# Attention in a one-core block kernel: PE's transposes, value products and halves of scores in another order at three places, two casts and one row scaling moved

## The chip, the cores and the metric

The kernel runs on one core of a Trainium2 chip. The metric is the device time of one execution in microseconds (us); of several executions the median is given. PE is the matmul engine (PEld its weight loads), DVE the vector engine, ACT the scalar engine, POOL and SP the two others; SP, POOL and ACT issue transfers. Each engine works through its own instructions in the order in which they were written, and waits on semaphores for the others.

## The reference

One layer of a block with two branches, for 1024 tokens of width 1024, in float32. What the change touches is the attention of branch A and the last product:

```python
h = rmsnorm(x, norm_g)
q, k, v, za, u, vs, zs, gm = split(h @ w_in)
q, k = partial_rope(q), partial_rope(k)            # 16 query heads, 2 key/value heads, 64 wide
s = einsum('bnqhgd,bnkhd->bhgnqk', qc, kb) / 8     # each chunk of 64 queries sees 192 keys
m = max(max(s), sink)
p = exp(s - m)
a = (p / (sum(p) + exp(sink - m))) @ vb            # 'bhgnqk,bnkhd->bnqhgd'
a = (a * silu(za)) @ w_att_out
sgo = (spatial_gating(gelu(u), gelu(vs)) * silu(zs)) @ w_sg_out
y = sigmoid(gm_a) * a + sigmoid(gm_s) * sgo
out = rmsnorm(x + y @ w_o, final_g)
```

## The kernel before

**The large products.** Every 1024-wide product is split two by two in Strassen's manner with seven partial products (weights' parts 0 to 6 against forms of the input called b11, t1, t2, b21, t3, b22, t4). Each float32 operand is held as a rounded high part and a rest (wh and wl for the weights; T_b11h, T_b11l and so on for the forms): ACT casts the high part (L174), DVE subtracts to get the rest (L175). One partial product (`product`, its matmuls at L388) is 12 matmuls of 128x512, three for each of four k. It takes a function `middle` that writes other work between k = 1 and k = 2. Accumulators lie in PSUM banks under four tags of two banks each: ps_mm, ps_o, ps_sc, ps_tp.

**Attention.** It has 32 steps (two key/value heads, eight blocks of 128 tokens, two parities). Eight locked pairs (`locked_pair`, p = 0 to 7) weave four steps each into the seven partial products of one pair of gate projections; the order of PE, ACT and DVE is there written out by hand and kept by the scheduler. In pair p the steps are called y and z (c and d of the pair before), then a, b, c, d. A step goes through these stages:

- `scores` (PE, L1196): two chunks of queries, each four matmuls of 128x192 into a ps_sc bank;
- `maxima` (DVE, L1221 to L1224), `exponentials` (ACT, L1231, L1240), `weigh` (DVE L1245 to L1252, ACT L1254): the normalised weights, tile pr;
- `turn` (PE): four transposes of the inner 128 keys (L1267) into one ps_tp bank, two of the outer 64-key ends (L1272) into another;
- `casts` (ACT, L1283, L1289), `inner_rest` (DVE, L1295), `ends_rest` (DVE, L1303): high parts and rests of the turned weights, tiles pT and pTb;
- `values` (PE, L1320): two matmuls of 128x512 with pT and two of 128x256 with pTb into a ps_o bank;
- `outputs` (ACT L1333, then DVE L1334): the result to tile aT, and from there to memory.

The pair begins with scores of a, turn of z, values of y on PE; then comes the b11 product, whose middle writes outputs of y, casts and rests of z, maxima and exponentials of a. Middle of t1: weigh a, values and outputs of z, the copy of the b11 accumulator to x11 (ACT, L1392), scores of b. The t2 product adds into that same accumulator, so it waits for the copy. Between t3 and b22: values of b, and then scores of d. At the end of a pair DVE adds t5 to x12 (L1471) and takes the rest of the next weights (L175), ahead of the next pair's outputs of y (L1334). Because only two ps_tp banks exist, the ends of z go into the bank that held the ends of y, and wait until `ends_rest` of y has read it.

In pairs 0 and 4 the first two steps belong to the first block of tokens, which has no earlier keys; their chunks are narrower. In pair 0 the scores of b come after the t1 product and not in its middle.

**The last product.** y @ w_o is done for four pairs of token tiles. Its seven forms are made from loaded quarters (tile bq) by `fill_b`; the last of them, t4, by two ACT casts T_t4h<-bq and two DVE rests. Around the same time `split_next` makes the weights' parts of the first token pair from tiles s and wr. PE first does the four b11 products, then, token pair by token pair, the other six.

**The last rows.** In the last token pair `last_by_halves` does the t4 product in two halves of 256 columns: each is added (L1810), squared and summed (ACT, L1812); then come the root, four short DVE operations (L147 to L152), the scaling and the stores. `scale_and_store(0)` scales the row tile that was finished before it: on ACT one half (L1835), on DVE the other (L1838), each followed by a store from SP.

Of the kernel before, what the change touches and what calls it, by code (L numbers as in the profile page):

```python
# [32 lines left out]
P = 128  # L33
# [3 lines left out]
HALF = 512  # L37
NT = S // P
HD = 64
# [15 lines left out]
def hybrid_tile(  # L55
# [29 lines left out]
    def bank(tag, dt=F32):  # L85
        return psum.tile([P, 512], dt, name=nm("ps_" + tag), tag="ps_" + tag, bufs=2)
# [46 lines left out]
    a_dr = scratch("a_dr")  # L133
    y_dr = scratch("y_dr")

    roots = []

    def stat():
        return mtile([P, 1], F32, "st1", 16)
# [27 lines left out]
    def split(hi, lo, src, minus=False):  # L167
        if minus:
            nc.scalar.mul(hi, src, -1.0)
            return nc.vector.scalar_tensor_tensor(  # L170
                lo, src, -1.0, hi.bitcast(F32), op0=ALU.mult, op1=ALU.subtract
            )
        else:
            nc.scalar.copy(hi, src)  # L174
            return nc.vector.tensor_sub(lo, src, hi.bitcast(F32))  # L175
# [198 lines left out]
    term = [None]  # L374
    LAST_OF_Q = 8

    def product(acc, part, form, fresh, middle=lambda: None, cols=slice(0, HALF)):
        wh, wl = part
        bh, bl = (v[:, :, cols] for v in form)
        for k in range(4):  # L380
            if k == 2:
                middle()
                half_done = mm
            ks = slice(k * P, (k + 1) * P)
            for n, (lt, rt) in enumerate(
                ((wh[:, ks], bh[:, k, :]), (wh[:, ks], bl[:, k, :]), (wl[:, ks], bh[:, k, :]))
            ):
                mm = nc.tensor.matmul(  # L388
                    acc,
                    lt,  # L390
                    rt,
                    start=fresh and k == 0 and n == 0,
                    stop=k == 3 and n == 2,
                    skip_group_check=True,
                )
        return half_done
# [410 lines left out]
    late = []  # L807
# [363 lines left out]
    def atile(shape, dt, tag, bufs):  # L1171
        return mtile(shape, dt, tag, bufs, pool)

    def window_of(t, c):

        return (64 * c, 64 * c + 192) if t else (P, P + 64 * (c + 1))
# [3 lines left out]
        first = (192, -64)[c]  # L1180
        return slice(first + lo, first + hi)

    def scores(n):

        g, t, par = steps[n]
        st = held[n] = SimpleNamespace(g=g, t=t, par=par)
        qt, kt = qT.pop(0), keys[g, t][0]
        q_of = qt[:].rearrange("p i (q c) -> p c (i q)", c=2)
        st.sc = []
        for c in range(2):  # L1190
            lo, hi = window_of(t, c)
            sc = bank("sc")[:].rearrange("p (i k) -> p i k", i=2)
            st.sc.append(sc)
            for i in range(2):
                for f in range(2):
                    nc.tensor.matmul(  # L1196
                        sc[:, i, lo:hi],
                        q_of[:, c, i * P : (i + 1) * P],
                        kt[:, f, lo:hi],
                        start=f == 0,  # L1200
                        stop=f == 1,
                    )
# [8 lines left out]
        st.pr = atile([P, 2, 384], F32, "pr", 2)  # L1211

    def sinks_of(st):
        return (v[:, 4 * st.g + st.par : 4 * st.g + st.par + 3 : 2] for v in (sink_sb, nsink_sb))
# [41 lines left out]
    def cols(c):  # L1256
        return slice(256 * c, 256 * c + 256)

    def turn(n):

        st = held[n]
        st.wide = wide = P if st.t else 64
        st.inner = bank("tp")
        for c in range(2):
            for i in range(2):
                at = (2 * c + i) * P
                nc.tensor.transpose(  # L1267
                    st.inner[0:wide, at : at + P], st.pr[:, i, place_of(c, 64 if st.t else P, 192)], ident[:]
                )
        st.ends = bank("tp")  # L1270
        for i in range(2):
            nc.tensor.transpose(st.ends[0:wide, i * P : (i + 1) * P], st.pr[:, i, P : P + wide], ident[:])  # L1272
# [30 lines left out]
            nc.vector.tensor_sub(st.b[lo, cols(c)], st.ends[hi, 0:256], st.b[hi, cols(c)].bitcast(F32))  # L1303

    def values(n):

        st = held[n]
        if st.par == 0:
            keys[st.g, st.t][3] = atile([P, 4, P], F32, "aT", 2)
        _, inner, ends, st.at = keys[st.g, st.t]  # L1310
        st.po = bank("o")
        vs = slice(st.par * HD, st.par * HD + P)
        if st.t:
            terms = [(inner[:, vs], st.a[:, i, :], slice(0, HALF)) for i in range(2)]
        else:
            terms = [(ends[:, 0, vs], st.a[:], slice(0, HALF))]
        for c in range(0 if st.t else 1, 2):
            terms.append((ends[:, c, vs], st.b[:, cols(c)], cols(c)))
        for i, (lt, rt, cs) in enumerate(terms):
            nc.tensor.matmul(  # L1320
                st.po[:, cs], lt, rt, start=i == 0, stop=i == len(terms) - 1, skip_group_check=True
            )

    def outputs(n):
# [22 lines left out]
    def locked_pair(p, finish):  # L1347
# [4 lines left out]
        def of(make, n, *rest):  # L1352
            if 0 <= n < len(steps):
                make(n, *rest)

        def multiply(acc, at, form, fresh, middle):
            pace[0] = product(acc, ready[n, at], hb[form], fresh, middle)
            part_of_early(1 if p < 5 else 2)

        n = done[0]  # L1360
# [26 lines left out]
        def h2():  # L1387
            of(weigh, a)
            of(values, z)
            of(outputs, z)  # L1390
            x11 = held["x11"] = xtile()
            nc.scalar.copy(x11[:], acc)  # L1392
# [378 lines left out]
    for p in range(4):  # L1771
# [30 lines left out]
        def last_by_halves():  # L1802

            nc.vector.tensor_add(xr[:, 2, :], xr[:, 2, :], acc)
            for c in range(2):
                cs = slice(c * 256, (c + 1) * 256)
                z = xr[:, 2, cs]
                half = bank("mm")[:, cs]
                product(half, ready[n, 6], ob["t4"], True, cols=cs)
                pace[0] = nc.vector.tensor_add(z, z, half)  # L1810
                ss = stat()
                nc.scalar.activation(bank("tp")[:, cs], z, AF.Square, accum_out=ss[:])  # L1812
                if c == 0:
                    sq[1] = based(ss, sq[1][0])
                else:
                    sq[1] = rstd_of(ss[:], 1.0 / D, sq[1])
            r = sq[1]
            row = slice((t + 1) * P, (t + 2) * P)
            v = scaled[1, 1][:]
            for c in range(2):  # L1820
                cs = slice(c * 256, (c + 1) * 256)
                z = xr[:, 2, cs]
                nc.vector.scalar_tensor_tensor(z, z, r[:], g_out[:, 0, cs], op0=ALU.mult, op1=ALU.mult)
                nc.scalar.mul(v[:, cs], v[:, cs], r[:])
                nc.sync.dma_start(out[row, cs], z)
                nc.scalar.dma_start(out[row, HALF + c * 256 : HALF + (c + 1) * 256], v[:, cs])

        def scale_and_store(i, p=p, t=t, xr=xr, sq=sq, scaled=scaled):
            r = sq[i]
            row = slice((t + i) * P, (t + i + 1) * P)  # L1830
            for e in range(2):
                z = xr[:, 2 * i + e, :]
                if (i, e) in scaled:
                    v = scaled[i, e][:]
                    nc.scalar.mul(v, v, r[:])  # L1835
                    nc.sync.dma_start(out[row, half_of(e)], v)
                    continue
                by_gain = nc.vector.scalar_tensor_tensor(z, z, r[:], g_out[:, e, :], op0=ALU.mult, op1=ALU.mult)  # L1838
# [137 lines left out]
```

## Time and profile before

| what | us |
|---|---|
| median of three runs | 921.0 (920.84 to 921.24) |
| the profiled execution | 921.45 |
| its span, first to last instruction | 919.7 |
| PE busy | 907.4 |
| DVE busy | 691.2 |
| ACT busy | 529.6 |
| the eight locked pairs, by PE's first scores of each | 332.6 to 562.7 |
| from one pair's scores to the next, pairs 2 and 3 | 29.5 |

The profile is one execution seen by the hardware. A row of its timeline has the start, the length, the engine, the source line, the operation, the tiles (out<-in), the shape and how many instructions were merged; in brackets stands idle time of the engine before it and what ended it. Matmuls overlap one another in these rows, since their ends are modelled: a 128x512 one is shown 0.39 long, but in an undisturbed run the next starts about 0.227 after it. So PE is read from start to start. The 1.7 us between the execution's time and its span lie before the first and after the last instruction.

### The profile page before, as it was taken

What the parts mean: (1) busy time and instruction counts of PE and PEld (TensorE: products, weight loads), DVE (VectorE), ACT (ScalarE), POOL (GpSimd) and SP (SyncE); (2) the same over time, 40 slices, a digit from 0 to 9 for tenths busy, and PEclk for the clock granted to TensorE, in tenths of its full rate; (3) what the DMA queues carried; (4) which work ended last, traced back from release to release, by engine and by line L of the source; (5) the groups of instructions that cost most, each with busy time, mean ns of one, the idle gap of its engine ahead of it and who ended that gap; (6) DMA issues with size and microseconds to landing.
All of it is one profiled execution on the core that took longest, in us unless ns stands there. A gap on an engine that the chain in (4) does not pass through costs nothing.

```text
span 919.7 us, 13199 instructions
## 1 busy us (share of the span) xinstructions
PE 907.4 (99%) x4296; PEld 749.4 (81%) x4296; DVE 691.2 (75%) x1233; ACT 529.6 (58%) x1058; POOL 141.9 (15%) x213
## 2 busy tenths in 40 slices
PE   8999999999999999999999999999999999999996
PEld 5888888888888888888888888888888888887885
DVE  6774776656678678777887788765599689579986
ACT  7942433334445456877778878444476475467443
POOL 1002222213011001222111110001110111210012
PEclk9999999999999999999999999999999999999999
DMA  7328788877788879999999994775568666998633
GB/s 241 122 97 217 172 150 185 177 186 212 242 270 260 270 249 328 266 241 260 255 344 246 266 246 144 284 252 179 173 204 304 226 206 179 282 322 271 206 115 114
DMA packets 129024, 206.10 MB, mean 224 GB/s; under 512 B 12634, under 2 KB 59738, under 8 KB 128956
## 3 DMA queue, kind: packets, MB, share of 16 engines
q1 hardware_dynamic: 107292, 146.27, 49.3%
q0 software_dynamic: 21376, 58.73, 27.2%
q8 instruction: 34, 0.56, 0.3%
q14 instruction: 34, 0.28, 0.1%
q10 hardware_dynamic: 288, 0.26, 0.1%
HBM read 148.46 MB, written 90.31 MB: 260 GB/s over the span
## 4 chain that ended last, share of the span: by engine, by line
PE 88%; DVE 4%; ACT 3%; DMA 3%; issue 1%; SPq 0%; ACTq 0%
PE ps_mm L388 40%; PE ps_o L388 24%; PE ps_mm L646 6%; PE ps_tp L388 4%; PE ps_sc L1196 2%; PE ps_o L1320 2%; PE ps_sc L388 2%; PE ps_tp L857 2%; PE ps_tp L646 1%; PE ps_sc L646 1%; PE ps_o L646 1%; PE ps_tp L1267 1%; ACT pr L1231 1%; PE ps_tp L1272 1%; ACT pr L1254 1%
## 5 line engine op out<-in xcount | busy, mean ns | idle before, releaser
L174 ACT CAST wh<-s 128x1024 fp32r<-128x1024 f32 (+1 forms) x78 | 77.9, 1002 | 78.9 <-PE ps_mm L388 25.4
L175 DVE TENSOR_TENSOR wl<-s,wh 128x1024 fp32r<-128x1024 f32 (+1 forms) x78 | 90.9, 1166 | 21.6 <-ACT wh L174 21.4
L175 DVE TENSOR_TENSOR wl<-wr,wh 128x1024 fp32r<-128x1024 f32 (+1 forms) x64 | 60.3, 944 | 53.0 <-ACT wh L174 53.0
L174 ACT CAST wh<-wr 128x1024 fp32r<-128x1024 f32 (+1 forms) x64 | 53.0, 829 | 77.2 <-PE ps_mm L388 33.7
L1231 ACT ACTIVATE pr<-ps_sc,sm 128x192 f32<-128x192 f32 (+2 forms) x128 | 51.2, 407 | 30.6 <-DVE sm L1222 22.0
L333 POOL DMA_DIRECT2D sums<-in_w_dram x48 | 36.6, 861 | 207.4 <-PE ps_mm L388 86.4
L388 PE MATMUL ps_o<-T_b22h,wh 128*128 128x512 f32 x148 | 59.3, 401 | 0.0
L388 PE MATMUL ps_o<-T_t1h,wl 128*128 128x512 f32 x148 | 58.0, 392 | 0.4 <-DVE wl L175 0.4
L388 PE MATMUL ps_o<-T_t1h,wh 128*128 128x512 f32 x148 | 58.3, 394 | 0.0
L388 PE MATMUL ps_o<-T_b22l,wh 128*128 128x512 f32 x148 | 57.8, 390 | 0.0
L388 PE MATMUL ps_o<-T_b22h,wl 128*128 128x512 f32 x148 | 57.7, 390 | 0.0
L388 PE MATMUL ps_o<-T_t1l,wh 128*128 128x512 f32 x148 | 57.7, 390 | 0.0
L388 PE MATMUL ps_mm<-T_t4h,wh 128*128 128x512 f32 (+1 forms) x144 | 55.8, 388 | 0.0
L388 PE MATMUL ps_mm<-T_t2h,wh 128*128 128x512 f32 x140 | 55.5, 396 | 0.0
L388 PE MATMUL ps_mm<-T_t4l,wh 128*128 128x512 f32 (+1 forms) x144 | 55.3, 384 | 0.0
L388 PE MATMUL ps_mm<-T_t4h,wl 128*128 128x512 f32 (+1 forms) x144 | 55.3, 384 | 0.0
L388 PE MATMUL ps_mm<-T_b11h,wh 128*128 128x512 f32 x140 | 55.2, 394 | 0.0
L388 PE MATMUL ps_mm<-T_t3h,wh 128*128 128x512 f32 x140 | 54.8, 391 | 0.0
L388 PE MATMUL ps_mm<-T_b11l,wh 128*128 128x512 f32 x140 | 54.7, 391 | 0.0
L388 PE MATMUL ps_mm<-T_b11h,wl 128*128 128x512 f32 x140 | 54.6, 390 | 0.0
L388 PE MATMUL ps_mm<-T_t3h,wl 128*128 128x512 f32 x140 | 54.6, 390 | 0.0
L388 PE MATMUL ps_mm<-T_t2h,wl 128*128 128x512 f32 x140 | 54.5, 390 | 0.0
(405 smaller groups left out, 2470.2 us busy)
## 6 DMA issues: line engine op xcount, KB each, us to landing
wr<-in_w_dram SPq DMA_DIRECT2D x80, 256.0 KB
sums<-in_w_dram POOLq DMA_DIRECT2D x24, 512.0 KB, 6.7
s<-sums SPq DMA_DIRECT2D x24, 512.0 KB
wr<-in_w_dram SPq DMA_DIRECT2D x16, 512.0 KB
q_hl<-qhl SPq DMA_DIRECT2D x16, 512.0 KB
q<-q_hl SPq DMA_DIRECT2D x64, 128.0 KB
y_dr<-x POOLq DMA_DIRECT2D x28, 256.0 KB, 6.5
sums<-in_w_dram POOLq DMA_DIRECT2D x24, 256.0 KB, 7.4
```

The source lines that it names most:

```text
L174: nc.scalar.copy(hi, src)
L175: return nc.vector.tensor_sub(lo, src, hi.bitcast(F32))
L333: return lambda: paced(nc.gpsimd.dma_start(dst, src, accum_op=op))
L388: mm = nc.tensor.matmul(acc, lt, rt, start=fresh and k == 0 and n == 0, stop=k == 3 and n == 2, skip_group_check=True,)
L646: mm = nc.tensor.matmul(acc, lt, rt, start=k == 0 and n == 0, stop=k == KC - 1 and n == 2)
L857: nc.tensor.matmul(pm[:, t * P : (t + 1) * P], xh[:, half * 4 + t, g * P : (g + 1) * P], bias[-1][1][:, g % 4, :], start=True, stop=True,)
L1196: nc.tensor.matmul(sc[:, i, lo:hi], q_of[:, c, i * P : (i + 1) * P], kt[:, f, lo:hi], start=f == 0, stop=f == 1,)
L1231: nc.scalar.activation(st.pr[:, i, place_of(c, lo, hi)], st.sc[c][:, i, lo:hi], AF.Exp, bias=st.nmax[:, c, i : i + 1], scale=-1.0, accum_o ...
L1254: nc.scalar.mul(v, v, st.inv[:, c, i : i + 1])
L1267: nc.tensor.transpose(st.inner[0:wide, at : at + P], st.pr[:, i, place_of(c, 64 if st.t else P, 192)], ident[:])
L1272: nc.tensor.transpose(st.ends[0:wide, i * P : (i + 1) * P], st.pr[:, i, P : P + wide], ident[:])
L1320: nc.tensor.matmul(st.po[:, cs], lt, rt, start=i == 0, stop=i == len(terms) - 1, skip_group_check=True)
```

## The change

At three places of a locked pair PE's instructions are put into another order; then two casts and one scaling are moved. No instruction is added or removed.

1. Start of a pair (pairs 1 to 7): turn of z and values of y are each cut in two, and the halves alternate: inner transposes of z, inner values of y, end transposes of z, end values of y.
2. Middle of t1 (pairs 1 to 7): the second chunk of scores of b moves from the middle to just before the last k, three matmuls later. The loads of queries that are issued with scores go with it.
3. After t3 (all pairs): the first chunk of scores of d moves between the inner and the end values of b. The second stays behind the end values.
4. The last product: the two casts T_t4h<-bq are ordered behind the cast of the weights that `split_next` made just before.
5. The last rows: `scale_and_store(0)` is called after the second half's sum instead of ahead of both halves.

The diff, with the cutting of `scores`, `turn` and `values` into two functions each left out where it only moves lines:

```diff
+            hi_casts.append(nc.scalar.copy(hi, src))
...
-    def product(acc, part, form, fresh, middle=lambda: None, cols=slice(0, HALF)):
+    def product(acc, part, form, fresh, middle=lambda: None, cols=slice(0, HALF), late=lambda: None):
...
+            if k == 3:
+                late()
...
+    def chunk_scores(n, c):
...
+        if c == 0:
+            held[n] = SimpleNamespace(g=g, t=t, par=par, q=qT.pop(0), sc=[])
...
+        if c == 0:
+            return
         if n + 3 < len(steps):
             qT.append(query_stage(*steps[n + 3]))
...
         of(scores, a)
-        of(turn, z)
-        of(values, y)
+        of(turn_inner, z)
+        of(inner_values, y)
+        of(turn_ends, z)
+        of(end_values, y)
...
             if p:
-                of(scores, b)
-
-        multiply(t5, 2, "t1", True, h2)
+                of(chunk_scores, b, 0)
+
+        def late2():
+            if p:
+                of(chunk_scores, b, 1)
+
+        multiply(t5, 2, "t1", True, h2, late2)
...
-        of(values, b)
+        of(inner_values, b)
+        of(chunk_scores, d, 0)
+        of(end_values, b)
         of(weigh, c)
...
-        of(scores, d)
+        of(chunk_scores, d, 1)
...
     split_next()
+    of_weights = hi_casts[-1]
     for _ in range(4):
         ob = next(fill)
+    for cast in hi_casts[-2:]:
+        after(cast, of_weights)
...
                 pace[0] = nc.vector.tensor_add(z, z, half)
+                if c:
+                    scale_and_store(0)
...
         by_b21()
-        scale_and_store(0)
         last_by_halves()
```

How PE's rows move at the start of pair 2 (place 1; ps_sc is scores of a, ps_tp the transposes of z, ps_o the values of y, ps_mm the b11 product). Before:

```order
L1196 MATMUL ps_sc_3651<-k_3373,q_3375 128x192 x4
L1267 MATMUL ps_tp_3664<-ident,pr_3575 128x128 x4
L1272 MATMUL ps_tp_3669<-ident,pr_3575 128x128 x2
L1320 MATMUL ps_o_3673<-pT_3608,vi_3359 128x512 x2
L1320 MATMUL ps_o_3673<-pTb_3610,v_3356 128x256 x2
L388 MATMUL ps_mm_3645<-T_b11h_143,wh_3553 128x512
```

Now:

```order
L1197 MATMUL ps_sc_3651<-k_3376,q_3378 128x192 x4
L1278 MATMUL ps_tp_3664<-ident,pr_3575 128x128 x4
L1338 MATMUL ps_o_3670<-pT_3608,vi_3359 128x512 x2
L1288 MATMUL ps_tp_3673<-ident,pr_3575 128x128 x2
L1346 MATMUL ps_o_3670<-pTb_3610,v_3356 128x256 x2
L390 MATMUL ps_mm_3645<-T_b11h_143,wh_3558 128x512
```

The two end transposes have moved behind the two inner value products. On DVE and ACT no instruction moves anywhere in the attention.

ACT's rows around the casts of form t4 in the last product (wh are weights' parts, g and x the copies out of PSUM). Before:

```order
L1758 COPY g_8159<-ps_sc_8158 128x512
L174 CAST T_t4h_8137<-bq_8134 128x1024
L174 CAST wh_8086<-s_8080 128x1024
L174 CAST wh_8090<-wr_8071 128x512
L174 CAST wh_8090<-s_8081 128x512
L174 CAST T_t4h_8137<-bq_8134 128x1024
L1758 COPY g_8174<-ps_mm_8173 128x512
L174 CAST wh_8119<-s_8081 128x512
L174 CAST wh_8119<-wr_8071 128x512
L1758 COPY g_8189<-ps_mm_8188 128x512
```

Now:

```order
L1795 COPY g_8159<-ps_sc_8158 128x512
L174 CAST wh_8086<-s_8080 128x1024
L174 CAST wh_8090<-wr_8071 128x512
L174 CAST wh_8090<-s_8081 128x512
L1795 COPY g_8174<-ps_mm_8173 128x512
L174 CAST wh_8119<-s_8081 128x512
L174 CAST wh_8119<-wr_8071 128x512
L174 CAST T_t4h_8137<-bq_8134 128x1024 x2
L1795 COPY g_8189<-ps_mm_8188 128x512
```

Both casts of t4 now stand behind all casts of the first token pair's weights, and still ahead of the fourth copy.

DVE's rows at the end (st are single columns for the root, bq the rows of the output). Before:

```order
L152 TENSOR_SCALAR st_1587_8782<-st_1586_8781,st_1585_8780 128x1
L1838 SCALAR_TENSOR_TENSOR bq_8675<-bq_8675,st_1587_8782,bq_8212 128x512
L1798 TENSOR_SCALAR st_1591_8810<-st_1589_8807,st_1578_8755 128x1
L1810 TENSOR_TENSOR bq_8675<-bq_8675,ps_mm_8814 128x256
L1799 TENSOR_SCALAR st_1592_8811<-st_1591_8810 128x1
L147 TENSOR_SCALAR st_1598_8833<-st_1594_8828,st_1592_8811 128x1
```

Now:

```order
L152 TENSOR_SCALAR st_1587_8782<-st_1586_8781,st_1585_8780 128x1
L1835 TENSOR_SCALAR st_1591_8806<-st_1589_8803,st_1578_8755 128x1
L1847 TENSOR_TENSOR bq_8675<-bq_8675,ps_mm_8810 128x256
L1836 TENSOR_SCALAR st_1592_8807<-st_1591_8806 128x1
L1877 SCALAR_TENSOR_TENSOR bq_8675<-bq_8675,st_1587_8782,bq_8212 128x512
L147 TENSOR_SCALAR st_1598_8833<-st_1594_8828,st_1592_8807 128x1
```

The scaling of the finished row (L1838, now L1877) stands behind the second half's sum (L1810, now L1847).

More of the change, by code (lines that the diff above doesn't have):

```diff
@@ L134, in hybrid_tile @@
     y_dr = scratch("y_dr")
-    roots = []
+    roots, hi_casts = [], []
     def stat():
@@ L173, in split @@
         else:
-            nc.scalar.copy(hi, src)
+            hi_casts.append(nc.scalar.copy(hi, src))
             return nc.vector.tensor_sub(lo, src, hi.bitcast(F32))
@@ L1181, in place_of @@
         return slice(first + lo, first + hi)
-    def scores(n):
+    def chunk_scores(n, c):
         g, t, par = steps[n]
[L1186 to L1202, printed above, removed]
+        if c == 0:
+            held[n] = SimpleNamespace(g=g, t=t, par=par, q=qT.pop(0), sc=[])
+        st, kt = held[n], keys[g, t][0]
+        q_of = st.q[:].rearrange("p i (q c) -> p c (i q)", c=2)
+        lo, hi = window_of(t, c)
+        sc = bank("sc")[:].rearrange("p (i k) -> p i k", i=2)
+        st.sc.append(sc)
+        for i in range(2):
+            for f in range(2):
+                nc.tensor.matmul(
+                    sc[:, i, lo:hi],
+                    q_of[:, c, i * P : (i + 1) * P],
+                    kt[:, f, lo:hi],
+                    start=f == 0,
+                    stop=f == 1,
+                )
+        if c == 0:
+            return
         if n + 3 < len(steps):
@@ L1211, in scores @@
         st.pr = atile([P, 2, 384], F32, "pr", 2)
+    def scores(n):
+        for c in range(2):
+            chunk_scores(n, c)
     def sinks_of(st):
@@ L1259, in turn, with turn_inner @@
     def turn(n):
+        turn_inner(n)
+        turn_ends(n)
+    def turn_inner(n):
         st = held[n]
@@ L1269, in turn, with turn_ends @@
                 )
+    def turn_ends(n):
+        st = held[n]
+        wide = st.wide
         st.ends = bank("tp")
@@ L1305, in values, with inner_values @@
     def values(n):
+        inner_values(n)
+        end_values(n)
+    def inner_values(n):
         st = held[n]
@@ L1313, in values, with end_values @@
         if st.t:
-            terms = [(inner[:, vs], st.a[:, i, :], slice(0, HALF)) for i in range(2)]
+            terms = [(inner[:, vs], st.a[:, i, :]) for i in range(2)]
         else:
-            terms = [(ends[:, 0, vs], st.a[:], slice(0, HALF))]
+            terms = [(ends[:, 0, vs], st.a[:])]
+        for i, (lt, rt) in enumerate(terms):
+            nc.tensor.matmul(st.po[:], lt, rt, start=i == 0, stop=False, skip_group_check=True)
+    def end_values(n):
+        st = held[n]
+        ends = keys[st.g, st.t][2]
+        vs = slice(st.par * HD, st.par * HD + P)
         for c in range(0 if st.t else 1, 2):
-            terms.append((ends[:, c, vs], st.b[:, cols(c)], cols(c)))
-        for i, (lt, rt, cs) in enumerate(terms):
             nc.tensor.matmul(
-                st.po[:, cs], lt, rt, start=i == 0, stop=i == len(terms) - 1, skip_group_check=True
+                st.po[:, cols(c)], ends[:, c, vs], st.b[:, cols(c)], start=False, stop=c == 1, skip_group_check=True
             )
@@ L1354, in of, with multiply @@
                 make(n, *rest)
-        def multiply(acc, at, form, fresh, middle):
-            pace[0] = product(acc, ready[n, at], hb[form], fresh, middle)
+        def multiply(acc, at, form, fresh, middle, late=lambda: None):
+            pace[0] = product(acc, ready[n, at], hb[form], fresh, middle, late=late)
             part_of_early(1 if p < 5 else 2)
```

## The prediction

> **What bounds the kernel now.** I read the page's fourth part, the chain that ended last, then the answer on waits for the locked pairs, then the chain of waits, then the timeline at each place of the change, and last the granted clock.
>
> ```profile
> PE 88%; DVE 4%; ACT 3%; DMA 3%; issue 1%; SPq 0%; ACTq 0%
> ```
>
> PE's own work sets the end nearly everywhere, and no matmul is removed. So the change can only take away gaps between PE's starts, and these are small. The waits of PE's weight loads between 330 and 575 us (columns: total us, times, longest) name three places, the three that the change reorders:
>
> ```profile
> PEld ps_tp L1272 <- issue: 2.0, 5, 0.4
> PEld ps_o L1320 <- ACT sm L1240: 2.0, 6, 0.3
> PEld ps_sc L1196 <- ACT pr L1231: 1.2, 6, 0.2
> ```
>
> These are waits of the loader, partly under a running matmul, so they are a bound and no sum. The chain of waits, asked for 355 to 450 us, says more. Between two of the five L1272 stops it runs through ACT and DVE alone:
>
> ```profile
> 363.60 0.59 ACT aT L1333
> ...
> 391.94 0.41 PE ps_tp L1272 x2
> ```
>
> From the outputs of y in pair 1 to the ends' rest of y that PE's end transposes await in pair 2 there are 28 us of ACT and DVE handing work to each other. So in this part PE is tied once per pair to a second clock, the loop of ACT and DVE. Whoever shortens only PE's side shortens nothing until the loop gets shorter too. This is the question for each edit.
>
> **Place 1, start of a pair.** Pair 2 in the timeline:
>
> ```profile
> 391.13 0.60 PE L1267 MATMUL ps_tp<-ident,pr 128*128 128x128 f32 x4
> 391.83 0.69 DVE L1471 TENSOR_TENSOR x<-x,ps_o 128x512 f32<-128x512 f32 x1
> 391.94 0.41 PE L1272 MATMUL ps_tp<-ident,pr 128*128 128x128 f32 x2 [0.22 <-DVE pTb L1303]
> 392.11 0.71 PE L1320 MATMUL ps_o<-pT,vi 128*128 128x512 f32 x2
> 392.43 1.22 DVE L175 TENSOR_TENSOR wl<-s,wh 128x1024 fp32r<-128x1024 f32 x1
> 393.09 0.58 ACT L1333 COPY aT<-ps_o 64x512 f32<-64x512 f32 x1 [0.91 <-PE ps_o L1320]
> 393.71 0.68 DVE L1334 TENSOR_TENSOR aT<-aT,ps_o 64x512 f32<-64x512 f32 x1
> ```
>
> The end transposes wait for DVE's ends' rest of y (L1303), which ends just before L1471 starts at 391.83. The four inner ones began at 391.13 and need 0.46 (as the scores of place 3 below, 0.93 / 8 = 0.116 each), so the others could have gone at 391.59: PE stands 0.35. In the new order the two inner value products, 2 x 0.23, fill that stop, and as they no longer come behind it, the values of y end about 0.45 sooner.
>
> What does that buy? The outputs (ACT L1333) start sooner, but the next link is DVE's L1334, and DVE is not free: behind the rest it has L1471 (391.83) and L175 (392.43). How soon L1334 can follow L175 is shown at the end of the section, where the same three DVE steps stand as at a pair's start and nothing else held it:
>
> ```profile
> 567.65 1.22 DVE L175 TENSOR_TENSOR wl<-s,wh 128x1024 fp32r<-128x1024 f32 x1
> 568.78 0.68 DVE L1334 TENSOR_TENSOR aT<-aT,ps_o 64x512 f32<-64x512 f32 x1
> ```
>
> That is 1.13 from start to start; in pair 2 it is 393.71 - 392.43 = 1.28. So the loop shortens by at most 0.15, not by 0.45, and by 0.03 if L1334 has to see the end of L175 (1.22) first. I take 0.13, nearer to the row that shows the pair of steps unheld. Five stops, 5 x 0.13 = **0.65**.
>
> One pair differs. Pair 4 has no earlier keys for two of its steps, and at the start of pair 5 DVE waits for PE's side:
>
> ```profile
> 480.44 0.68 DVE L1334 TENSOR_TENSOR aT<-aT,ps_o 64x512 f32<-64x512 f32 x1 [0.34 <-ACT aT L1333]
> ```
>
> There up to 0.34 of PE's gain from pair 4 comes through; less some 0.1 for switches that pair 4 now makes without a wait to hide them: **0.25**.
>
> **Place 2, scores of b.**
>
> ```profile
> 397.02 0.62 PE L1320 MATMUL ps_o<-pT,vi 128*128 128x512 f32 x2
> 397.72 1.35 PE L1196 MATMUL ps_sc<-k,q 128*128 128x192 f32 x8
> 398.91 0.42 PE L388 MATMUL ps_o<-T_t1h,wh 128*128 128x512 f32 x1
> 400.32 0.59 ACT L1392 COPY x<-ps_mm 128x512 f32<-128x512 f32 x1
> 400.96 0.50 PE L388 MATMUL ps_mm<-T_t2h,wh 128*128 128x512 f32 x1
> ```
>
> Eight scores take 1.19 here (397.72 to 398.91), against 0.93 in place 3 (412.63 to 413.56): 0.26 of waiting for the exponentials of a to free the bank. The three matmuls between fill it. But six matmuls and six transposes later the t2 product starts at 400.96, 0.05 after ACT's copy to x11 ends (400.91): PE is caught there, and the copy hangs on the loop. I cost place 2 at **0**; the cover is that copy, and if it came sooner the six waits would give at most 6 x 0.26 = 1.6. The second chunk, 0.6 later, is read by DVE's maxima only after L1334; query loads issued with it are for three steps on.
>
> **Place 3, values of b and scores of d.**
>
> ```profile
> 411.78 0.62 PE L1320 MATMUL ps_o<-pT,vi 128*128 128x512 f32 x2
> 412.63 1.09 PE L1196 MATMUL ps_sc<-k,q 128*128 128x192 f32 x8
> 413.56 0.41 PE L388 MATMUL ps_o<-T_b22h,wh 128*128 128x512 f32 x1
> ```
>
> From 411.78 to 412.63 values take 0.85, against 0.70 where nothing holds them (397.02 to 397.72). The 0.15 goes, but PE carries it only to the next pair's end transposes, where the rest of y decides. In the last pair nothing waits for it any more: **0.1**. The new switches in pair 1 and the last cost as much: **-0.1**. Together the attention gives 0.65 + 0.25 + 0.1 - 0.1 = **0.9**. Ends: a loss of 0.2 if DVE gains nothing and switches count; 2.6 if PE's 0.45 came through at all five stops.
>
> A rule speaks against this part. The Trainium skill, "TensorE: Matmul & The Clock Gate", section "A second HAM failure mode: psum-queue depth-cycling", says that cycling through PSUM banks makes PE pause between groups so often that its clock gate swings between half and full rate. The change adds bank changes; it is rival 3 below.
>
> **The casts.**
>
> ```profile
> 841.36 0.68 DVE L1691 SCALAR_TENSOR_TENSOR s<-s,wr 128x512 f32<-128x512 f32 x1
> 843.73 1.05 ACT L174 CAST T_t4h<-bq 128x1024 fp32r<-128x1024 f32 x1 [2.37 <-DMA bq<-g]
> 844.68 1.04 ACT L174 CAST wh<-s 128x1024 fp32r<-128x1024 f32 x1
> 845.76 1.22 DVE L175 TENSOR_TENSOR wl<-s,wh 128x1024 fp32r<-128x1024 f32 x1 [1.98 <-ACT wh L174]
> 846.20 0.40 PE L388 MATMUL ps_o<-T_t1l,wh 128*128 128x512 f32 x1
> 847.04 0.50 PE L388 MATMUL ps_o<-T_t1h,wl 128*128 128x512 f32 x1 [0.44 <-DVE wl L175]
> 847.38 0.39 PE L388 MATMUL ps_o<-T_t1h,wh 128*128 128x512 f32 x1
> ```
>
> ACT stands idle for a load of t4's source, with the weights' cast behind it, though s was done at 841.36 + 0.68 = 842.04. In the new order that cast runs 842.1 to 843.1, DVE, idle for 1.98 ahead of 845.76, takes the rest at about 843.8, and it ends by 845.1. PE wants it at 846.43 and finds it: 847.04 - 846.43 = 0.61, and the restart after the stop (847.38 - 847.04 = 0.34 for 0.23) gives 0.11: 0.72. DVE is then 1.5 or more ahead, which also removes the next such stop:
>
> ```profile
> 863.27 0.39 PE L388 MATMUL ps_o<-T_t1l,wh 128*128 128x512 f32 x1
> 863.53 0.50 PE L388 MATMUL ps_o<-T_t1h,wl 128*128 128x512 f32 x1
> ```
>
> 0.26 for a step of 0.23, and the same restart of 0.11: 0.14. Sum **0.86**. The price: t4's casts now come at about 847.3 to 849.3, behind the weights' casts, which wait for a buffer until the b11 products end near 846. Their reader, DVE's rest of t4, stands nine DVE steps behind the weights' first rest (845.76 before), each of some 0.6 to 1.2, so I expect room. Ends: 0 (if the buffer for the first cast is not free at 842) and 0.9.
>
> **The last rows.**
>
> ```profile
> 912.20 0.28 PE L388 MATMUL ps_mm<-T_t4h,wl 128*128 128x256 f32 x1
> 912.24 0.75 DVE L1838 SCALAR_TENSOR_TENSOR bq<-bq,st,bq 128x512 f32<-128x512 f32 x1
> 912.29 0.72 ACT L1835 ACTIVATE g<-g,st 128x512 f32<-128x512 f32 x1 [0.25 <-DVE st L152]
> 913.03 0.41 DVE L1810 TENSOR_TENSOR bq<-bq,ps_mm 128x256 f32<-128x256 f32 x1
> 913.47 0.39 ACT L1812 ACTIVATE ps_tp<-bq 128x256 f32<-128x256 f32 x1 [0.46 <-DVE bq L1810]
> 914.01 0.21 DVE L147 TENSOR_SCALAR st<-st,st 128x1 f32<-128x1 f32 x1 [0.51 <-ACT ps_tp L1812]
> ```
>
> PE's last matmul ends at 912.20 + 0.28 = 912.48, and its sum could start at about 912.52; it runs at 913.03, since L1838 stands before it. Moved behind, it lets the square start at about 912.98 (ACT's L1835 ends at 913.01) for 913.47. L1838 then runs 912.95 to 913.70, where DVE waits anyway (0.51 ahead of L147); it delays L147 by under 0.2, which ACT's root next to it covers. I take **0.45**; ends 0 and 0.5. Its store goes out 0.7 later, still over a microsecond ahead of the last ones.
>
> **Sum.** 0.9 + 0.86 + 0.45 = 2.2. The profiled execution took 921.45, so it becomes 919.25; it lies 0.45 above the median of 921.0, which becomes **918.8**.
>
> **Rivals.**
>
> 1. *PE's side comes through* (0.13): DVE's L1471 and L175 turn out not to hold L1334. For it: ACT stands 0.91 idle ahead of L1333 at 393.09. Against: DVE's start to start of 1.28 in pair 2 is full already. 5 x 0.45 + 0.25 + 1.31 = 3.8: 917.2.
> 2. *The attention's waits only move* (0.20): the ends' rest, the x11 copy and the loop take back all, and the edit there does nothing that it says. For it: PE's starts at 391.94 and 400.96 both follow the awaited step within 0.14. Only 0.86 + 0.45 = 1.3 remain: 919.7.
> 3. *Slower* (0.04): PE's granted clock falls in the attention, as its groups get shorter and change banks more often. The row of the 201.7 us from pair 1 on:
>
> ```profile
> 361.00:562.70 201.70, 200.56 (x1078) 169.13 (x1077) 163.39 (x402) 157.11 (x460) 39.35 (x51) 1.00 0.98 261
> ```
>
> The granted clock (third from the end) is 1.00 with ten bank changes a pair already, which speaks against it. It decides below 2.2 / 201.7, a mean of 0.989; at 0.97 it costs 6.2, so 921.0 + 6.2 - 2.2 = 925.0. This is what the skill's rule on cycling would make of it; the trace does not agree with the rule so far.
>
> 4. *The casts give nothing* (0.05): the buffer of the first weights' cast is not free at 842. 0.9 + 0.45: 919.65.
>
> **How the numbers follow.** My forecast has 0.58, with 0.5 either way. About 0.2% (1.8 us, so 919.2) is what a measurement of this kernel tells from no change. Of the forecast three quarters lie below 919.2, and all of rival 1: 0.57. Rivals 2 and 4 and the rest of the forecast lie within 0.2%: 0.38; slower 0.05. The range reaches to rival 1 and past rival 2: 917.0 to 920.1.
>
> **What would show it.** Right: no stop ahead of the end transposes, yet pairs 2 and 3 still about 29.35 apart, L1334 at 1.13 to 1.15 behind L175; t2 still 0.05 behind the x11 copy; no PE stops near 846 and 863; the last square about 0.5 nearer to PE's end. Wrong: pairs at 29.0 (rival 1) or 29.5 (rival 2), the rest still late at 846, or a granted clock under 1.00.

## The result and the profile after

| | median us | lowest to highest, runs |
|---|---|---|
| before | 921.02 | 920.62 to 921.96, 8 |
| changed | 918.99 | 916.94 to 920.57, 8 |

The ratio is 0.9979, with an interval of 0.997 to 0.9989: 1.0 to 2.8 us less, 2.0 by the medians. The forecast was 918.8.

The profiled execution of the changed kernel took 916.94, the lowest of its eight. So the two profiles lie 4.5 apart, and the stages have to be separated before anything is read from them. The marks are starts of PE's rows; pair 0 stands apart, since it took 25.6 to 26.4 in kernels that don't differ there. (PE's first scores of pair 0 start at 335.34 before; the 332.6 and 562.7 in the table further up are the starts of t4 products, so they are no marks of the pairs. The distances there are right.)

| stage, us | before | changed | less |
|---|---|---|---|
| up to PE's first scores of pair 0 | 335.34 | 333.39 | 1.95 |
| pair 0 | 25.77 | 25.59 | 0.18 |
| attention: first scores of pair 1 to the last end values | 210.23 | 209.28 | 0.95 |
| from there to PE's end (the casts lie here) | 341.14 | 340.21 | 0.93 |
| PE's end to the end of the span | 7.20 | 6.68 | 0.52 |

The first line is no part of the change: nothing before pair 0 was edited, and over all fourteen profiles of this study the first scores come between 333.39 and 337.16. What is left is 2.6 in this pair of profiles.

The chain that ended last, in the page of the changed kernel (share of the span by engine):

```profile
PE 84%; DVE 6%; ACT 5%; DMA 3%; issue 1%; SPq 0%; ACTq 0%
```

It was 88%, 4% and 3% before. PE was stopped less, yet a larger share of the chain runs through DVE and ACT. The waits of the locked pairs (330 to 575 us; total, times, longest) show where:

```profile
PEld ps_mm L390 <- ACT x L1420: 3.2, 6, 0.7
PE ps_mm L390 <- ACT x L1420: 1.6, 4, 0.4
PEld ps_tp L1288 <- issue: 1.3, 5, 0.3
```

The five waits of the end transposes on DVE (1.0 us of PE's own) and the six of the scores of b on ACT are gone from the list. In their place PE waits for ACT's copy of x11, which had been 0.2 us in one wait of the loader. Place 1 in pair 2, from the timeline:

```profile
388.89 0.60 PE L1278 MATMUL ps_tp<-ident,pr 128*128 128x128 f32 x4
389.25 0.71 PE L1338 MATMUL ps_o<-pT,vi 128*128 128x512 f32 x2
389.82 0.41 PE L1288 MATMUL ps_tp<-ident,pr 128*128 128x128 f32 x2
390.31 1.22 DVE L175 TENSOR_TENSOR wl<-s,wh 128x1024 fp32r<-128x1024 f32 x1
390.31 0.39 PE L390 MATMUL ps_mm<-T_b11h,wh 128*128 128x512 f32 x1
390.51 0.58 ACT L1359 COPY aT<-ps_o 64x512 f32<-64x512 f32 x1 [0.48 <-PE ps_o L1346]
391.44 0.67 DVE L1360 TENSOR_TENSOR aT<-aT,ps_o 64x512 f32<-64x512 f32 x1
```

In the kernel before, the first inner transpose of this pair starts at 391.13, and its b11 product here:

```profile
392.89 0.40 PE L388 MATMUL ps_mm<-T_b11h,wh 128*128 128x512 f32 x1
```

From the first inner transpose to the b11 product PE needs 1.42 (388.89 to 390.31), 1.76 before (391.13 to 392.89); in only_p1, further down, it is 1.36, so hardly a stop is left. ACT's output is done at 391.09, but DVE's part of it (L1360) starts at 391.44, which is 1.13 behind L175: DVE, busy with L175, is the one that holds it. And place 2, in the same pair:

```profile
396.32 0.60 PE L1197 MATMUL ps_sc<-k,q 128*128 128x192 f32 x4
397.91 0.38 PE L1288 MATMUL ps_tp<-ident,pr 128*128 128x128 f32 x2
398.02 0.59 ACT L1420 COPY x<-ps_mm 128x512 f32<-128x512 f32 x1
398.66 0.50 PE L390 MATMUL ps_mm<-T_t2h,wh 128*128 128x512 f32 x1 [0.37 <-ACT x L1420]
```

The scores of b no longer stop. PE comes to t2 sooner and stands there, until 0.05 after the copy ends (398.61), as before. The casts and the last row, from the timeline of ACT, DVE and PE:

```profile
839.00 1.05 ACT L174 CAST wh<-s 128x1024 fp32r<-128x1024 f32 x1 [0.72 <-DVE s L1725]
840.61 1.23 DVE L175 TENSOR_TENSOR wl<-s,wh 128x1024 fp32r<-128x1024 f32 x1
843.34 0.39 PE L390 MATMUL ps_o<-T_t1h,wl 128*128 128x512 f32 x1
843.56 0.39 PE L390 MATMUL ps_o<-T_t1h,wh 128*128 128x512 f32 x1
843.95 1.99 ACT L174 CAST T_t4h<-bq 128x1024 fp32r<-128x1024 f32 x2
848.69 1.24 DVE L175 TENSOR_TENSOR T_t4l<-bq,T_t4h 128x1024 fp32r<-128x1024 f32 x1
...
908.51 0.42 DVE L1847 TENSOR_TENSOR bq<-bq,ps_mm 128x256 f32<-128x256 f32 x1 [0.19 <-PE ps_mm L390]
908.92 0.74 DVE L1877 SCALAR_TENSOR_TENSOR bq<-bq,st,bq 128x512 f32<-128x512 f32 x1
908.97 0.39 ACT L1851 ACTIVATE ps_tp<-bq 128x256 f32<-128x256 f32 x1
909.57 0.21 DVE L147 TENSOR_SCALAR st<-st,st 128x1 f32<-128x1 f32 x1
```

The weights' rest ends at 841.84, 1.5 ahead of its reader at 843.34, and PE runs through in steps of 0.22 to 0.23. The casts of t4 end at 845.94; their reader on DVE starts at 848.69, so nobody waits. At the end the sum starts 0.03 after PE's last matmul ends (908.48), 0.55 before; the square and the scaling run beside one another.

### The profile page after: what moved, and what is told of

It is laid out like the page before. It is cut to its first block, busy times and chain, and to the rows that moved or that the text cites. A ratio compares the mean times of both kernels' runs of the same rounds, so it can differ in the third digit from the quotient of the medians.

```text
span 915.2 us, 13187 instructions
## 1 busy us (share of the span) xinstructions
PE 903.2 (99%) x4296; PEld 748.7 (82%) x4296; DVE 691.7 (76%) x1233; ACT 530.5 (58%) x1058; POOL 142.0 (16%) x213
## 4 chain that ended last, share of the span: by engine, by line
PE 84%; DVE 6%; ACT 5%; DMA 3%; issue 1%; SPq 0%; ACTq 0%
PE ps_mm L390 38%; PE ps_o L390 24%; PE ps_mm L648 6%; PE ps_tp L390 4%; PE ps_sc L390 2%; PE ps_tp L859 2%; PE ps_sc L1197 1%; ACT pr L1238 1%; DVE sm L1228 1%; PE ps_tp L648 1%; PE ps_sc L648 1%; PE ps_o L648 1%; ACT pr L1261 1%; DVE pTb L1319 1%; DMA q<-q_hl 1%
## 5 line engine op out<-in xcount | busy, mean ns | idle before, releaser
L175 DVE TENSOR_TENSOR wl<-s,wh 128x1024 fp32r<-128x1024 f32 (+1 forms) x78 | 91.1, 1168 | 20.3 <-ACT wh L174 20.0
L175 DVE TENSOR_TENSOR wl<-wr,wh 128x1024 fp32r<-128x1024 f32 (+1 forms) x64 | 60.6, 948 | 53.4 <-ACT wh L174 53.4
```

## The experiments

Twelve kernels, each timed in five to eleven executions beside the kernel before: only_... is the kernel before with that one part of the change, the others are the changed kernel with the edits shown below. "Pair 2" is the distance from PE's first scores of pair 2 to those of pair 3; the stages are those of the table above. A total carries the changing time up to pair 0, some 1 us either way for a median of five, so effects of less are read from the stages.

| kernel | median us | ratio to before, interval | pair 2 | attention | to PE's end | tail |
|---|---|---|---|---|---|---|
| before | 921.02 | | 29.50 | 210.23 | 341.14 | 7.20 |
| changed | 918.99 | 0.9979 (0.997 to 0.9989) | 29.32 | 209.28 | 340.21 | 6.68 |
| only_p1 | 920.4 | 0.9995 (0.9986 to 1.0004) | 29.37 | 209.25 | 340.93 | 7.19 |
| only_p2 | 920.98 | 1.0003 (0.9994 to 1.0012) | 29.52 | 210.39 | 340.71 | 7.20 |
| only_p3 | 920.81 | 0.9999 (0.9991 to 1.0008) | 29.51 | 210.48 | 340.20 | 7.19 |
| only_casts | 920.78 | 0.9997 (0.9988 to 1.0005) | 29.47 | 210.40 | 340.25 | 7.19 |
| only_tail | 920.6 | 0.9997 (0.9988 to 1.0006) | 29.55 | 210.33 | 340.91 | 6.69 |
| early | 918.73 | 0.9977 (0.9968 to 0.9986) | 29.33 | 209.00 | 340.21 | 6.68 |
| maxb | 915.63 | 0.9947 (0.9933 to 0.996) | 28.81 | 206.46 | 340.17 | 6.69 |
| maxb_early | 913.56 | 0.9925 (0.9913 to 0.9938) | 28.47 | 204.32 | 340.22 | 6.68 |
| me_none | 915.41 | 0.9939 (0.9927 to 0.9952) | 28.71 | 205.96 | 340.22 | 6.69 |
| me_no1 | 914.4 | 0.9931 (0.9918 to 0.9943) | 28.47 | 204.31 | 340.22 | 6.69 |
| me_no2 | 916.71 | 0.9945 (0.9931 to 0.9958) | 28.70 | 205.75 | 340.24 | 6.69 |
| me_no3 | 914.58 | 0.9929 (0.9917 to 0.9942) | 28.48 | 204.46 | 340.22 | 6.68 |

**One place at a time.** Place 1 alone, in the kernel before:

```diff
-        of(turn, z)
-        of(values, y)
+        of(turn_inner, z)
+        of(inner_values, y)
+        of(turn_ends, z)
+        of(end_values, y)
```

> The kernel before with place 1 alone (start of a pair: inner transposes of z, inner values of y, end transposes of z, end values of y). Theory (the loop of ACT and DVE limits the pair): the stop of 0.35 ahead of the end transposes is gone, but pairs 2 and 3 still take 29.36 (29.50 before) and pair 4 some 27.9 (28.15 before), in all 0.9 less: 920.1. Rival, PE's side comes through: pairs 2 and 3 take 29.05, in all 2.5 less: 918.5. Rival, the waits only move: 29.5, 921.0.

Pair 2 took 29.37, pair 3 29.34 and pair 4 27.73; attention 209.25, where the three kernels with an unchanged attention (before, only_casts, only_tail) have 210.23 to 210.40. That is 1.0 to 1.15 less, for 0.9 forecast; the total alone, with an interval that holds 1, would not have shown it. The timeline of pair 2 shows the second clock at work:

```profile
397.26 0.61 PE L1197 MATMUL ps_sc<-k,q 128*128 128x192 f32 x4
398.14 0.72 PE L1197 MATMUL ps_sc<-k,q 128*128 128x192 f32 x4 [0.27 <-ACT pr L1238]
398.69 0.41 PE L390 MATMUL ps_o<-T_t1h,wh 128*128 128x512 f32 x1
```

The scores of b take 1.43 (397.26 to 398.69) for 0.93 of work, a stop of 0.50, where it was 0.26. At the start of the pair PE saves 0.40 (1.36 from the first inner transpose, 391.07, to the b11 product, 392.43; 1.76 before). Of that it waits 0.24 more here; the rest, 0.16, is near the 0.13 by which the pair became shorter.

Place 2 alone:

```diff
-                of(scores, b)
-
-        multiply(t5, 2, "t1", True, h2)
+                of(chunk_scores, b, 0)
+
+        def late2():
+            if p:
+                of(chunk_scores, b, 1)
+
+        multiply(t5, 2, "t1", True, h2, late2)
```

> The kernel before with place 2 alone (second chunk of the scores of b three matmuls later). Theory: no gain, pairs 2 and 3 stay at 29.5, and the 0.26 saved stand as a stop of PE of 0.2 to 0.3 at the start of the t2 product, until ACT's copy of x11 ends: 921.0. Rival, the stop's time is gained: 6 x 0.26 = 1.6, pairs at 29.24, 919.4.

In the kernel before, the t2 product of pair 2 starts at 400.96, and the two end transposes ahead of it here:

```profile
400.76 0.38 PE L1272 MATMUL ps_tp<-ident,pr 128*128 128x128 f32 x2
```

With place 2:

```profile
401.42 0.59 ACT L1420 COPY x<-ps_mm 128x512 f32<-128x512 f32 x1
401.57 0.38 PE L1288 MATMUL ps_tp<-ident,pr 128*128 128x128 f32 x2
402.06 0.51 PE L390 MATMUL ps_mm<-T_t2h,wh 128*128 128x512 f32 x1
```

From the first of the two transposes to t2 it takes 0.49, where it was 0.20: a stop longer by 0.29, about the 0.26 that the scores no longer wait, and it ends 0.05 behind the end of the copy at 402.01. Pair 2 stays at 29.52. Place 3 alone:

```diff
-        of(values, b)
+        of(inner_values, b)
+        of(chunk_scores, d, 0)
+        of(end_values, b)
...
-        of(scores, d)
+        of(chunk_scores, d, 1)
```

> The kernel before with place 3 alone (first chunk of the scores of d between the inner and the end values of b). Theory: the 0.15 of PE's wait ahead of the end values goes, but the pairs with a stop at the next start (2, 3, 6) keep 29.5; only where no such stop follows (pairs 0, 1, 5 and 7) up to 0.15 each may show: 920.4 to 921.0. Rival, the time is gained in every pair: 29.35 in pairs 2 and 3 as well, 7 x 0.15 = 1.05, 919.9.

```profile
390.79 0.62 PE L1278 MATMUL ps_tp<-ident,pr 128*128 128x128 f32 x4
391.74 0.41 PE L1288 MATMUL ps_tp<-ident,pr 128*128 128x128 f32 x2 [0.33 <-DVE pTb L1319]
```

Pairs 1 and 5 became 0.14 and 0.15 shorter, as thought (the 0.18 of pair 0 shows nothing: it takes 25.61 in only_tail too, where it is unchanged). But in pair 2 PE then stands 0.14 longer at the next end transposes (0.95 from start to start here, 0.81 before), and pairs 3 and 4 took 0.27 and 0.14 more: over the attention nothing is left. In pair 3 of this kernel, and in the same pair of the changed one, PE also waits 0.22 at the inner transposes. In these two, and in maxb, ACT's scaling of the weights (L1261) waited once for DVE's L1259 instead of running beside it; why only there is open.

**The loop.** Two edits that leave PE's order alone. In the first ACT takes the copy of x11 where it was idle:

```diff
             of(exponentials, a, 0)
-            of(exponentials, a, 1)
 
         multiply(acc, 0, "b11", True, h0)
+        x11 = held["x11"] = xtile()
+        nc.scalar.copy(x11[:], acc)
+        of(exponentials, a, 1)
...
             of(outputs, z)
-            x11 = held["x11"] = xtile()
-            nc.scalar.copy(x11[:], acc)
```

> The changed kernel, and ACT's copy of x11 taken ahead of the second half of the exponentials of a, where ACT stood idle for 0.76; PE's order is untouched. Theory (the loop of ACT and DVE is the pair's second clock): PE's stop at the start of t2 (0.37 in pair 2) is gone, but it comes back as a stop later in the pair, at the transposes of b, and pairs 2 and 3 keep 29.2 to 29.3 (29.32 in the changed kernel): 918.5 to 919.0. Rival, this copy is what holds PE: six pairs gain 0.35 each, pairs 2 and 3 take 28.97, 2.1 less than the changed kernel: 916.9.

```profile
400.43 0.48 PE L390 MATMUL ps_mm<-T_t2h,wh 128*128 128x512 f32 x1
...
405.51 0.55 DVE L1259 TENSOR_SCALAR pr<-pr,sm 128x192 f32<-128x192 f32 x2
405.57 0.80 ACT L1261 ACTIVATE pr<-pr,sm 128x192 f32<-128x192 f32 x2 [0.50 <-DVE sm L1253]
405.97 0.78 PE L1278 MATMUL ps_tp<-ident,pr 128*128 128x128 f32 x4 [0.38 <-DVE pr L1259]
```

The stop at t2 is gone, and 5.5 us later PE stands 0.38 at the transposes of b, which wait for the weights (L1259, L1261). Pairs 2 and 3 take 29.33 and 29.31. A stop of 0.37 was taken away, and its whole length came back at the next meeting.

The second edit touches DVE's order alone (the small tiles of a step are also made with its first chunk instead of its second):

```diff
-            of(outputs, z)
-            x11 = held["x11"] = xtile()
-            nc.scalar.copy(x11[:], acc)
             if p:
                 of(chunk_scores, b, 0)
+                of(maxima, b, 0)
+            of(outputs, z)
+            x11 = held["x11"] = xtile()
+            nc.scalar.copy(x11[:], acc)
...
-        of(maxima, b, 0)
+        if p == 0:
+            of(maxima, b, 0)
         of(maxima, b, 1)
```

> The changed kernel, and on DVE alone the maxima of b's first chunk moved ahead of its part of the outputs of z, into 0.95 us in which DVE waits for ACT; PE's and ACT's orders are untouched. Theory (loop of ACT and DVE): ACT's exponentials of b come 0.6 to 1.0 sooner, the loop gets shorter, and PE gains though nothing of its own changed: pairs 2 and 3 take 29.0 to 29.1 (29.32 in the changed kernel), 0.8 to 1.2 less in all, 917.8 to 918.2. Rival, the loop is not what limits: pairs stay at 29.3, 919.0.

```profile
392.99 0.68 DVE L1360 TENSOR_TENSOR aT<-aT,ps_o 64x512 f32<-64x512 f32 x1 [0.46 <-ACT aT L1359]
...
398.58 0.55 DVE L1228 TENSOR_REDUCE sm<-ps_sc 128x2 f32<-128x384 f32 x1
399.60 0.59 ACT L1423 COPY x<-ps_mm 128x512 f32<-128x512 f32 x1
399.61 0.69 DVE L1360 TENSOR_TENSOR aT<-aT,ps_o 64x512 f32<-64x512 f32 x1 [0.29 <-ACT aT L1359]
400.08 0.43 ACT L1238 ACTIVATE pr<-ps_sc,sm 128x192 f32<-128x192 f32 x1
400.24 0.50 PE L390 MATMUL ps_mm<-T_t2h,wh 128*128 128x512 f32 x1
```

ACT's exponentials of b follow right behind the copy (399.60, then 400.08); in the changed kernel ACT stood idle for 0.99 between the copy, which ended at 398.61, and these:

```profile
399.60 0.42 ACT L1238 ACTIVATE pr<-ps_sc,sm 128x192 f32<-128x192 f32 x1 [0.99 <-DVE sm L1229]
```

And at the start of the pair (392.99) DVE's L1360 now waits 0.46 for ACT and PE, where it was late by itself: the loop is ahead of PE there. Pair 2 takes 28.81, 0.51 less, twice what was expected, and the total is 3.4 below the changed kernel, for 0.8 to 1.2 expected. The theory had the direction right, and its size was an estimate that was too small. Both edits together:

> The changed kernel with both: the maxima of b's first chunk ahead of the outputs of z on DVE, and the copy of x11 ahead of the second exponentials of a on ACT. Theory: with the loop shorter, the copy of x11 is what PE meets next, so the two together give more than the sum of each alone (at most 0.3 and some 1.0): pairs 2 and 3 at 28.8 to 28.9, 2.0 to 2.5 less than the changed kernel, 916.5 to 917.0. Rival, the two edits give what they give alone: 917.7.

Pair 2 at 28.47, 913.56: 0.9925 of before (0.9913 to 0.9938). That is again more than was expected (28.8 to 28.9, and 916.5 to 917.0). Early alone gave nothing on its own; behind maxb it gives 0.34 a pair, as the copy of x11 is then the last thing PE meets. The chain that ended last, in the page of this kernel:

```profile
PE 97%; DVE 1%; DMA 1%; ACT 0%; SPq 0%; issue 0%; ACTq 0%
```

and its windows row for the attention from pair 1 on, but for its last few us (the length of the window comes first, then PE's busy time; the granted clock is third from the end):

```profile
360.47:554.00 193.53, 193.53 (x1065) 166.77 (x1064) 162.06 (x400) 156.69 (x461) 38.58 (x50) 1.00 1.01 270
```

PE's rows leave no gap in all 193.53 us of it. This is the best version of the study.

**The three places again, with the loop out of the way.** In maxb_early each place was put back as it was before the change, and all three together (the same lines as in the diffs above, the other way round; casts and last row stay changed).

> The kernel with the maxima of b and the copy of x11 moved (maxb_early), and all three places of PE's order put back as they were before the change; casts and last row as in the changed kernel. Theory (the stops of before were made by the loop, which is shorter now): only the scores of b still wait for the exponentials of a, 0.1 to 0.2 a pair, and the switches of banks that the new orders add are saved; pairs 2 and 3 take 28.45 to 28.65 (28.47 with the new orders), 913.5 to 914.8. Rival, the stops are PE's own (0.35, 0.26 and 0.15 a pair as before): pairs take 29.2, 919.

> maxb_early with place 1 alone put back. Theory: the rest of y's ends ends at 389.70 there and PE's inner transposes end at 390.3, so the end transposes wait for nothing and pairs 2 and 3 stay at 28.4 to 28.5: 913.5. Rival: the stop of 0.35 comes back, pairs at 28.8, 915.5.

> maxb_early with place 2 alone put back. Theory: ACT's last exponential of a that frees the bank ends near 396.5, when PE would want it for the second chunk of the scores of b; a stop of 0.1 to 0.2 a pair, pairs 2 and 3 at 28.5 to 28.65, 913.9 to 914.8. Rival: 0.26 or more as before, pairs at 28.73 and 915.3; or none, 913.5.

> maxb_early with place 3 alone put back. Theory: the rest of b's ends ends at 409.04, PE wants it at 410.0, so nothing waits and pairs 2 and 3 stay at 28.4 to 28.5: 913.5. Rival: 0.15 a pair as before, pairs at 28.62, 914.6.

Pair 2 took 28.47 without place 1, 28.48 without place 3, 28.70 without place 2, and 28.71 without all three. So the worths are turned round: place 1, which alone paid in the change, is worth nothing here, and place 2, which was worth nothing there, is worth 0.23 a pair. In the waits of me_none (total, times, longest) there is one kind left of the three that stood in the profile before:

```profile
PEld ps_sc L1197 <- ACT pr L1238: 1.1, 6, 0.2
```

The scores of b wait for the bank that ACT's exponentials of a read, in all six pairs. That is a tie of its own between PE and ACT within a pair. The stops at the end transposes and at the values of b were only the loop being late. The expectation had 0.1 to 0.2 a pair for place 2, a little low, and the medians of all four lie above what was expected, by 0.6 to 1.9; part of that is the time up to pair 0 (337.16 in me_no2's profile, the latest of all).

**The casts and the last row alone.**

```diff
+    of_weights = hi_casts[-1]
     for _ in range(4):
         ob = next(fill)
+    for cast in hi_casts[-2:]:
+        after(cast, of_weights)
```

> The kernel before with the casts alone (both casts of t4 behind the casts of the first token pair's weights). Theory: PE's stops near 846 and 863 (0.72 and 0.14) are gone and nothing is paid: 0.86 less, 920.1. Rival, the casts of t4 come late for their own product: a new stop of PE at t4, and no gain, 921.0 or more.

```diff
                 pace[0] = nc.vector.tensor_add(z, z, half)
+                if c:
+                    scale_and_store(0)
...
-        scale_and_store(0)
         last_by_halves()
```

> The kernel before with the last row's scaling alone behind the second half's sum. Theory: from PE's last matmul to the last instruction 6.7 us, 7.2 before: 0.5 less, 920.5. Rival, the later store of the finished row is what ends last then: 7.2 or more, 921.0 or more.

Only_tail has a tail of 6.69, as expected. Only_casts has no stop near 846 and 863, also as expected, and the stage takes 340.25. Its total came out at 920.78 for 920.1 expected, 0.3 below the median of 921.06 beside it, with an interval that holds 1. But the kernels that kept the old order of casts show that the stop is not always there. ACT's cast of t4 in only_p2 and in only_p3:

```profile
844.51 1.05 ACT L174 CAST T_t4h<-bq 128x1024 fp32r<-128x1024 f32 x1 [1.94 <-DMA bq<-g]
846.54 1.23 DVE L175 TENSOR_TENSOR wl<-s,wh 128x1024 fp32r<-128x1024 f32 x1 [1.54 <-ACT wh L174]
847.41 0.39 PE L390 MATMUL ps_o<-T_t1l,wh 128*128 128x512 f32 x1
847.82 0.50 PE L390 MATMUL ps_o<-T_t1h,wl 128*128 128x512 f32 x1
```

```profile
842.45 1.05 ACT L174 CAST T_t4h<-bq 128x1024 fp32r<-128x1024 f32 x1 [1.05 <-DMA bq<-g]
844.48 1.23 DVE L175 TENSOR_TENSOR wl<-s,wh 128x1024 fp32r<-128x1024 f32 x1 [0.66 <-ACT wh L174]
846.46 0.39 PE L390 MATMUL ps_o<-T_t1h,wl 128*128 128x512 f32 x1
```

In only_p2 the rest ends at 847.77 and PE starts 0.05 later: 0.41 after the matmul ahead, a stop of 0.18. In only_p3 ACT waited 1.05 for the load instead of 1.94, the rest ended at 845.71, 0.75 ahead of PE, and there was no stop. How much is lost is best read from the whole t1 products, which take 2.72 each where nothing stops them (only_casts, only_p3). The two together took 0.91 more in the profile before, 0.74 in only_p1 and in only_tail, 0.51 in only_p2 and nothing in only_p3: 0.58 on the mean.

That the load decides it can be read from the same five profiles. The cast that waits for it starts ahead of PE's first matmul of t1 by 2.24 in the kernel before, 2.43 in only_p1 and only_tail, 2.67 in only_p2 and 3.55 in only_p3. The first t1 product took 0.75, 0.56, 0.56, 0.32 and 0 too long: in the four with a stop, the lead and the loss add up to 2.99 each time.

## Why the prediction was right

- **What bounds the kernel.** That PE is tied to a second clock of ACT and DVE in the locked pairs is shown from three sides: PE's stops moved on, whole or for the most part (only_p1, only_p2, early), an edit of DVE's order alone made the pairs 0.51 shorter (maxb), and two of the three kinds of stop vanish when the loop is shorter, with PE's old order (me_no1, me_no3). "PE's own work sets the end nearly everywhere" was said too broadly: the page's 88% is a mean over the span, and hides that in the attention PE was not alone: of the 201.7 us from pair 1 on, at least 46 of the chain lay on ACT and DVE.
- **Place 1, 0.65 + 0.25.** Right by mechanism and size. At the five starts with a stop (pairs 2, 3, 4, 6 and 7) DVE's part of the output came 1.27 to 1.28 behind L175 before, and 1.13 to 1.14 in only_p1 and in the changed kernel; only_p1 gains 1.0 to 1.15 in the attention. Pairs 2, 3 and 6 gained 0.13 to 0.15 and pair 4 0.42, against 0.13 and 0.13 + 0.25. The values of y were to end 0.45 sooner; it was 0.40, and only rival 1 and the upper end of 2.6 were built on that.
- **Place 2, nothing.** Right in only_p2, and so was the cover: the copy of x11.
- **Place 3 and the switches, 0.1 - 0.1.** The sum was right, the way to it too simple. The 0.15 shows in pairs 1 and 5 and is given back in pairs 3 and 4. So pair 3 of the changed kernel took 29.59, and the sign that was named, pairs 2 and 3 about 29.35 apart, came true for pair 2 alone (29.32). A price of switches does not show: with and without places 1 and 3, pair 2 takes 28.47 and 28.48, and the start of the pair takes 1.36 in both orders (maxb_early, me_no1).
- **The casts, 0.86.** The mechanism was right; the term was too large by 0.3, because it was read from one execution, in which the load came later for PE than in the four others; the mean of five is 0.58. The change would have gained nothing on only_p3's execution, though not for the reason of rival 4: in the changed kernel the cast of the weights starts as soon as s is done (839.00), so its buffer was free.
- **The last row, 0.45.** It gave 0.51.
- **The sum.** 1.0 for the attention, 0.6 and 0.5 make 2.1, and the medians differ by 2.0, with 1.0 to 2.8 as the interval. That 918.99 lies within 0.2 of 918.8 is in part luck: the casts' term was 0.3 too large, the attention's 0.1 too small, and the interval is wider than both.
- **Rivals.** Rival 1 wanted pairs at 29.0; they took 29.32 and 29.59. Once the loop is shorter, a stop of PE's own does come through, yet that of place 2 and not that of place 1. Rival 2 is out for place 1 by only_p1's attention, and holds for places 2 and 3. Rival 4 is out, as said. Rival 3: the granted clock stayed at 1.00 in the attention of the changed kernel (third from the end), although PE's output tile changes 25 times from one pair's scores to the next, 19 before; the prediction's ten was too few:

```profile
359.00:560.65 201.65, 199.82 (x1082) 169.44 (x1081) 163.91 (x406) 158.44 (x466) 39.47 (x51) 1.00 0.97 260
```

The Trainium skill's section on cycling ("TensorE: Matmul & The Clock Gate", "A second HAM failure mode: psum-queue depth-cycling") describes swings of the clock for bf16 groups of 512 columns; for the float32 groups of this kernel neither this trace nor that of maxb_early shows them.

## What to carry to other kernels

Where an in-order engine stops at several places of a loop, ask first whether the stops are its own or one late partner met again and again: take one away, and see if another grows by the same amount. If it does, shorten the partner's chain, best by moving work of a lightly waiting engine into its idle gaps, and only then mend the stops that remain; their worth can turn round. Read a stop that hangs on a transfer from several executions, not from one.

## What the runs showed beside this

The part of the program up to pair 0, the same in all kernels, took 333.39 to 337.16 in fourteen profiles; what makes that spread was not followed up. It is larger than the whole effect of the change, so totals of single executions, and single profiles compared by their spans, say little here: 4.5 between the two profiles against 2.0 between the medians.
